# Strassen units in a half of the up-projection, late loads on GpSimd's queue and the gate's sigmoid at the pair's end, in a one-core decoder layer on Trainium2

## The chip, the cores and the metric

The kernel runs on one core of a Trainium2 chip. A core has five engines that run side by side, each with its own queue of instructions: TensorE (PE in the profile; PEld is its loading of weights) multiplies matrices, VectorE (DVE) and ScalarE (ACT) work element by element, GpSimd (POOL) does small odd jobs, and SyncE (SP) only starts transfers. Sixteen DMA engines move data between HBM and the on-chip memory SBUF; both SP and POOL start such transfers here. Matmul results land in the accumulator memory PSUM, in banks of 512 columns. The metric is the device time of one execution, in microseconds, as the median of several runs.

## What is computed

One layer of a decoder trunk in fp32, with 512 tokens and a model width of 2048. The part that matters here is the middle line of this excerpt, the up-projection of two branches with their gates:

```python
h = rmsnorm(x, attn_norm_g[i])
proj = h @ w_in[i]                        # u | v_sgu | q | k | v_att | g_a | g_b
...
y_a = chunked_spatial_gating(u, v_sgu, w_s[i], b_s[i]).reshape(B, S, SGU_WIDTH)
...
y_b = stick_breaking_attention(q, k, v_att).reshape(B, S, SB_WIDTH)

merged = jax.nn.sigmoid(g_a) * (y_a @ w_up_a[i]) + jax.nn.sigmoid(g_b) * (y_b @ w_up_b[i])
x = x + merged @ w_o[i]

h = rmsnorm(x, ffn_norm_g[i])
hid = h @ w_ffn_in[i]
...
x = x + (jax.nn.silu(gate) * up) @ w_ffn_out[i]

ple = p[i] @ w_ple[i]
x = x + jax.nn.sigmoid(rmsnorm(x, ple_norm_g[i]) @ w_ple_gate[i]) * ple
```

`y_a` and `y_b` are 1024 wide, the gates `g_a` and `g_b` 2048 wide. The row factor of the first norm is left out of the in-projection's operands and multiplied into its results afterwards.

## The kernel before

**Data layout.** Everything is transposed: features stand on the 128 partitions, the 512 tokens along the columns. A block of 256 features is held as 1024 columns (two halves of 512). Each fp32 operand is split into a high part `hi` (rounded on ScalarE, L286 for operands, L359 for weights) and a low part `lo` (the rest, on VectorE, L287 and L356), and a product is three matmuls, high by high, high by low and low by high (`mm3`, L289 to L298).

**Units and pairs.** A *unit* is one 256 by 256 block of weights against one operand block. A *pair* (`pair`, L807, and class `Pair`) makes one 256-feature block of output, summed over all units; `doubles` takes units two at a time. A unit is of one of two kinds. Kind "P" (plain) multiplies the four 128 by 128 blocks directly, 12 matmuls of 512 columns, into two PSUM banks, y and z. Kind "S" is one Strassen step (in Winograd's form) over feature halves and token halves: seven products of three matmuls with 256 columns each, 21 in all, into four banks; `mix` (L709) combines the products on ScalarE and VectorE. With `doubled` set, and no P unit in the pair, a different order of the S products is used, with 512 columns in two of the three terms (L687 to L694).

**Weights.** `plan` lists the weights in the order of use, `Weights` brings them. A landing buffer (four of them) receives each entry by SP (L339 for P, L341 and L343 for S). An S entry of two units comes as 256 KB and 384 KB; GpSimd then adds a further 256 KB onto it while loading (L363, an accumulating load); VectorE makes two more sums (L375), and both engines split the blocks. `prepare_early` and `prepare_late` run these steps for entries one to four ahead of the one in use.

**Operands.** A `Form` is an operand block on its way from a raw load to its split parts. `plain_form` (L613) holds the two parts for P units alone. `late_form` (L599) first builds what P units need (`plain_first`, L532) and later, from a second load of the same block, the sums and differences that S units need. Two arenas in SBUF, `parts` (split operands, eight *places* of 3584 columns and 1024 more) and `wholes` (raw blocks), give out space by hand with `take` and `give`. `now` (L830) turns an S unit into a P unit while the output index j is below that unit's entry in a bounds list; so the first pairs of a stage run plain, until the second loads are in.

**The order of the work.** `tick` (L209) is called every one or two units while TensorE's instructions are written out: at each tick at most one operand load is asked for, one form is begun, one second load is asked for, and the callbacks put off by `after(n, ...)` run. What a tick writes is held behind the latest matmuls on its engine, and each engine and each queue executes in the order written.

**The stages.** The in-projection (eight operand forms that fill all places) makes in turn q, k, v and 14 of the 16 gate blocks, with the attention's steps between, then the spatial gating's blocks s and u, then the last gate blocks a7 and b7. Each gate block is stored raw to HBM (`gate_spill`, L1327). `y_b` is stored too (`y_spill`); `y_a` stays in `wholes`. The up-projection (L1350 to L1374) runs j = 0 to 7, and for each j first the b half, then the a half, four P units each. It loads the gate block by SP, scales it by the norm's row (`scaled`, L1222) and takes the sigmoid (L1357) one tick after the pair begins, and multiplies the pair's two banks into it (L1362). The sum of both halves is stored as "mix". Between the j come pairs for the embeddings (`ple_pair`). Then follow the output projection (`w_o`), the FFN's two projections and the last gate. Their operands are spilled to HBM between stages and come back through `spilled_form` (L1338), all with `load` (L516) on SP's queue.

The two places of the code that the change's parts turn on:

```python
        for b in "ba":
            plan((w_up_a if b == "a" else w_up_b)[j], "PPPP")      # L1276
...
            after(1, gate)                                          # L1359
            pr = pair([ys[b, i] for i in range(4)], last=j == KU - 1)
            for h, ps in zip((g[:, :T], g[:, T:]), pr.ends()):
                nc.vector.tensor_tensor(out=h, in0=h, in1=ps, op=ALU.mult)
```

## Time and profile before

| What | Value |
|---|---|
| Median of 3 runs | 2661.22 us (2660.4 to 2664.61) |
| Profiled execution, its time | 2659.74 us |
| Profiled execution, its span | 2658.0 us |
| Granted TensorE clock, mean | 0.999 |
| DMA traffic | 559.77 MB, mean 211 GB/s |

How to read the profile: its page gives the busy time of each engine, the chain of work that ended last followed back from the end, and the costliest groups of instructions. A row such as `L356 DVE TENSOR_TENSOR wlo<-wholes,whi ... x22 | 26.9, 1223 | 29.8 <-ACT whi L359 29.7` is a group: source line, engine, operation, what it writes and reads, count, busy us, mean ns of one, then the time its engine stood idle just before, and for whom. A view of waits says who waited for whom, in us, with the number of times and the longest one. A view by stretches gives busy time and counts between two moments; an instruction that began before the stretch is counted in it too. Matmuls are pipelined: each lasts longer than the step from one start to the next, so TensorE's pace is read from starts.

### The profile page before, as it was taken

The numbers are of one execution on the slowest core, as the hardware profiler recorded it, in microseconds if no ns is written. First come the engines' busy times: TensorE is split into PE (matmuls) and PEld (weight loads), VectorE is DVE, ScalarE is ACT, GpSimd is POOL, SyncE is SP. The second block draws the span as 40 slices with busy tenths as digits, with TensorE's granted clock in tenths as the row PEclk, the third lists the DMA queues.
The fourth block names the chain that finished last, engine by engine and source line by source line (L and its number), as shares of the span: only waits on it lengthen the run. The fifth ranks groups of instructions, "written<-read, shape, count | busy, mean of one in ns | idle before, by whom it ended". The sixth has DMA issues, their size and how long they took to land.

```text
span 2658.0 us, 42554 instructions
## 1 busy us (share of the span) xinstructions
PE 2638.2 (99%) x15336; PEld 2312.3 (87%) x15336; DVE 2234.6 (84%) x3821; ACT 1403.2 (53%) x2233; POOL 448.1 (17%) x556
## 2 busy tenths in 40 slices
PE   8999999999999999999999999999999999999999
PEld 7888888888998888888888888888888888889898
DVE  8687878787886558999888888888889989989876
ACT  7756565655554334566444444444445445455543
POOL 0122222232220001101111111111110211211110
PEclk9999999999999999999999999999999999999999
DMA  7677777777775668978888888788887989978884
GB/s 229 162 194 171 192 173 191 172 191 179 178 191 183 232 212 268 265 236 218 223 210 216 206 200 203 194 209 204 199 207 221 257 227 273 229 229 260 256 240 123
DMA packets 293459, 559.77 MB, mean 211 GB/s; under 512 B 26368, under 2 KB 140544, under 8 KB 293248
## 3 DMA queue, kind: packets, MB, share of 16 engines
q1 hardware_dynamic: 231136, 441.95, 50.7%
q0 software_dynamic: 62112, 115.11, 27.5%
q8 instruction: 120, 1.97, 0.3%
q14 instruction: 91, 0.75, 0.1%
HBM read 505.57 MB, written 51.38 MB: 210 GB/s over the span
## 4 chain that ended last, share of the span: by engine, by line
PE 90%; DVE 4%; DMA 3%; issue 1%; ACT 1%; SPq 0%; POOL 0%; ACTq 0%; POOLq 0%; DVEq 0%
PE ps L692 53%; PE ps L298 10%; PE ps L297 9%; PE ps L296 9%; PE small L692 6%; DVE wlo L356 1%; DVE wholes L527 1%; DMA wholes<-w_ffn_out 1%; PE small L1103 1%; PE small L1155 1%; DVE parts L287 1%; PE small L1029 1%; DMA x<-wholes 1%; ACT whi L359 0%; PE small L1214 0%
## 5 line engine op out<-in xcount | busy, mean ns | idle before, releaser
L692 PE MATMUL ps<-parts,whi 128*128 128x512 f32 x4200 | 1409.4, 398 | 1.6 <-DVE out L796 1.0
L359 ACT ACTIVATE whi<-wholes 128x512 fp32r<-128x512 f32 (+2 forms) x940 | 871.5, 941 | 745.8 <-DVE wholes L375 286.6
L356 DVE TENSOR_TENSOR wlo<-wholes,whi 128x512 fp32r<-128x512 f32 (+2 forms) x940 | 979.4, 1076 | 73.7 <-ACT whi L359 73.0
L692 PEld LDWEIGHTS ps<-parts,wlo 128*128 128x128 f32 x4200 | 790.2, 188 | 178.2 <-issue 1.9
L692 PE MATMUL ps<-parts,wlo 128*128 128x256 f32 x4200 | 831.3, 279 | 0.9 <-DVE wlo L356 0.9
L692 PEld LDWEIGHTS ps<-parts,whi 128*128 128x128 f32 x4200 | 677.1, 189 | 10.5 <-issue 3.6
L297 PE MATMUL ps<-parts,whi 128*128 128x256 f32 (+1 forms) x1832 | 605.0, 331 | 0.7 <-DVE parts L287 0.5
L298 PE MATMUL ps<-parts,wlo 128*128 128x256 f32 (+1 forms) x1832 | 604.9, 331 | 0.5 <-DVE wlo L356 0.5
L296 PE MATMUL ps<-parts,whi 128*128 128x256 f32 (+1 forms) x1816 | 597.3, 330 | 7.4 <-ACT parts L286 5.3
L297 PEld LDWEIGHTS ps<-parts,whi 128*128 128x128 f32 x1832 | 347.0, 189 | 39.0 <-DVE parts L287 2.7
L296 PEld LDWEIGHTS ps<-parts,whi 128*128 128x128 f32 x1816 | 343.6, 190 | 40.4 <-ACT parts L286 5.7
L298 PEld LDWEIGHTS ps<-parts,wlo 128*128 128x128 f32 x1832 | 347.3, 190 | 32.4 <-DVE wlo L356 1.6
L375 DVE TENSOR_TENSOR wholes<-wholes 128x256 f32<-128x256 f32 (+1 forms) x820 | 345.0, 421 | 17.9 <-DVE wlo L356 1.4
L751 DVE TENSOR_TENSOR out<-out,ps 128x256 f32<-128x256 f32 x490 | 202.3, 416 | 147.6 <-ACT out L748 147.4
L363 POOL DMA_DIRECT2D wholes<-w_ffn_in x169 | 147.1, 870 | 702.1 <-DVE wholes L375 251.7
L363 POOL DMA_DIRECT2D wholes<-w_in x132 | 116.6, 885 | 531.3 <-DVE wholes L375 132.8
L692 PE MATMUL small<-parts,whi 128*128 128x512 f32 x480 | 190.3, 397 | 0.0
L287 DVE TENSOR_TENSOR parts<-wholes,parts 128x1024 fp32r<-128x1024 f32 (+3 forms) x137 | 122.8, 907 | 18.5 <-ACT parts L286 18.5
L286 ACT ACTIVATE parts<-wholes 128x1024 fp32r<-128x1024 f32 (+3 forms) x137 | 106.5, 800 | 54.2 <-DVE wholes L527 35.7
L748 ACT ACTIVATE out<-ps 128x256 f32<-128x256 f32 x258 | 96.3, 383 | 50.7 <-PE ps L692 46.7
L363 POOL DMA_DIRECT2D wholes<-w_ffn_out x64 | 55.7, 871 | 360.6 <-DMA wholes<-w_ffn_out 89.2
L1402 ACT ACTIVATE out<-out 128x512 f32<-128x512 f32 x44 | 27.9, 633 | 155.6 <-DVE out L1401 155.6
(124 smaller groups left out, 1770.0 us busy)
## 6 DMA issues: line engine op xcount, KB each, us to landing
wholes<-w_ffn_in SPq DMA_DIRECT2D x169, 384.0 KB, 5.5
wholes<-w_in SPq DMA_DIRECT2D x132, 384.0 KB, 5.1
wholes<-w_ffn_in SPq DMA_DIRECT2D x169, 256.0 KB, 4.7
wholes<-w_ffn_in POOLq DMA_DIRECT2D x169, 256.0 KB, 5.3
wholes<-w_in SPq DMA_DIRECT2D x132, 256.0 KB, 4.3
wholes<-w_in POOLq DMA_DIRECT2D x132, 256.0 KB, 5.0
wholes<-w_ffn_out SPq DMA_DIRECT2D x64, 384.0 KB, 6.3
wholes<-x SPq DMA_DIRECT2D x45, 512.0 KB, 5.8
```

Of the source, the lines that this page charges most:

```text
L286: return (nc.scalar.activation(hi, src, AF.Copy), nc.vector.tensor_tensor(out=lo, in0=src, in1=hi.bitcast(F32), op=ALU.subtract))
L287: nc.vector.tensor_tensor(out=lo, in0=src, in1=hi.bitcast(F32), op=ALU.subtract))
L296: nc.tensor.matmul(ps, sh, mh, start=start, stop=False)
L297: nc.tensor.matmul(ps, sh, ml, start=False, stop=False)
L298: return nc.tensor.matmul(ps, sl, mh, start=False, stop=stop)
L356: in_turn(nc.vector.tensor_tensor(out=self.lo[:, blocks], in0=r, in1=h.bitcast(F32), op=ALU.subtract))
L359: in_turn(nc.scalar.activation(h, r, AF.Copy))
L363: nc.gpsimd.dma_start(out=raw[:, 3:5], in_=self.src[:, 1:3], accum_op=ALU.add)
L375: in_turn(nc.vector.tensor_tensor(out=o, in0=x, in1=y, op=ALU.add))
L692: m = nc.tensor.matmul(out, l, r, start=first and k == 0, stop=last and k == 1)
L748: in_turn(nc.scalar.activation(out, x, AF.Copy, scale=scale))
L751: in_turn(nc.vector.tensor_tensor(out=out, in0=x, in1=y, op=op))
```

## The change

1. `w_up_b`'s units become Strassen units after the first one or two j (`UP_UNTIL`), and y_b's forms `late_form`. For j = 0 the order is a, then b; from j = 1 on b, then a, as before.
2. Gate blocks are scaled by the norm's row two ticks after their pair, before the spill. The sigmoid is written at the end of the up pair. A pair with S units is multiplied in from SBUF in one operation.
3. The loads of gate blocks, of y_b and of all spilled operands (first and second ones) go by GpSimd's queue.
4. Space is given back earlier: the attention's tiles after the last spatial-gating block, the norm's row three ticks into the up-projection. The first part of y_a's first form lies in the 1024 columns at the top of `parts`.

```diff
+UP_UNTIL = 1, 1, 2, 2
...
-    def load(src, n=1024, how="old"):
+    def load(src, n=1024, how="old", queue=nc.sync):
         b = take(n, how)
-        nc.sync.dma_start(out=b.f(0, 1024), in_=src)
+        queue.dma_start(out=b.f(0, 1024), in_=src)
...
     def plain_form(src, ready=always, gain=None, raw=1024, how="low", far=False):
+        hows = [how] * 2 if isinstance(how, str) else how
+
         def steps(form):
-            hi, lo = form.blocks = parts.take(1024, how), parts.take(1024, how)
+            hi, lo = form.blocks = [parts.take(1024, h) for h in hows]
...
                 op0=ALU.mult, op1=ALU.add)
+        if rnd == 3:
+            assert ("b", 3) in y_done
+            give(*att.values())
+            att.clear()
...
         for j in range(KU):
-            for b in "ba":
-                plan((w_up_a if b == "a" else w_up_b)[j], "PPPP")
+            for b in "ba" if j else "ab":
+                plan((w_up_a if b == "a" else w_up_b)[j],
+                     "PPPP" if b == "a" else now("SSSS", UP_UNTIL, j))
...
     def y_form(c, i):
-        return plain_form((lambda: y_a[i]) if c == "a" else lambda: load(y_spill[i]),
-                          lambda: len(y_done) == 8, raw=0 if c == "a" else 1024,
-                          far=c == "b")
-
-    ys = {(c, i): y_form(c, i) for c in "ba" for i in range(4)}
+        def ready():
+            return len(y_done) == 8
+
+        if c == "a":
+            return plain_form(lambda: y_a[i], ready, raw=0, how="low" if i else ("high", "low"))
+        return late_form(lambda size=1024: load(y_spill[i], size, queue=nc.gpsimd), ready, far=True)
+
+    ys = {(c, i): y_form(c, i) for c in "ab" for i in range(4)}
...
-            d = tc.dram_tile([P, 1024], F32, name=nm("gsp"))
-            nc.sync.dma_start(out=d, in_=o)
-            gate_spill[w, i] = d
-    finish_waiting()
-    give(*att.values())
+            d = gate_spill[w, i] = tc.dram_tile([P, 1024], F32, name=nm("gsp"))
+
+            def spill_gate(o=o, d=d):
+                scaled(o, row1)
+                nc.sync.dma_start(out=d, in_=o)
+
+            after(2, spill_gate)
+    after(3, lambda: give(norm1.block))
...
     def spilled_form(kind, n, j, gain=None, **how):
         return (late_form if kind == "S" else plain_form)(
-            lambda size=1024: load(spill[n, j], size), lambda: (n, j) in there, gain, far=True,
+            lambda size=1024: load(spill[n, j], size, queue=nc.gpsimd), lambda: (n, j) in there, gain, far=True,
             **how)
...
     for j in range(KU):
-        for b in "ba":
-            s = load(gate_spill[b, j], 1024, "low")
+        for b in "ba" if j else "ab":
+            s = load(gate_spill[b, j], 1024, "low", nc.gpsimd)
             g = s.f()
-
-            def gate(g=g):
-                scaled(g, row1)
-                nc.scalar.activation(g, g, AF.Sigmoid)
-
-            after(1, gate)
-            pr = pair([ys[b, i] for i in range(4)], last=j == KU - 1)
-            for h, ps in zip((g[:, :T], g[:, T:]), pr.ends()):
-                nc.vector.tensor_tensor(out=h, in0=h, in1=ps, op=ALU.mult)
-            if b == "b":
+            pr = pair([ys[b, i] for i in range(4)], last=j == KU - 1, j=j,
+                      until=UP_UNTIL if b == "b" else None)
+            nc.scalar.activation(g, g, AF.Sigmoid)
+            if pr.n["S"]:
+                tt(g, g, pr.out(), ALU.mult)
+            else:
+                for h, ps in zip((g[:, :T], g[:, T:]), pr.ends()):
+                    tt(h, h, ps, ALU.mult)
+            if j not in part:
                 part[j] = s
...
-    give(norm1.block)
```

More of the change, by code (lines that the diff above doesn't have):

```diff
@@ L630, in steps @@
             yield
-        return Form("P", steps, [(parts, 1024, how)] * 2 + [(wholes, raw, "low")] * bool(raw),
+        return Form("P", steps, [(parts, 1024, h) for h in hows] + [(wholes, raw, "low")] * bool(raw),
                     ready, src, far)
```

## The prediction

> **What bounds the kernel now.** I read the page's busy line and chain of waits first, then busy time by stretches, then who made TensorE wait.
>
> ```profile
> PE 2638.2 (99%) x15336; PEld 2312.3 (87%) x15336; DVE 2234.6 (84%) x3821; ACT 1403.2 (53%) x2233; POOL 448.1 (17%) x556
> ...
> PE 90%; DVE 4%; DMA 3%; issue 1%; ACT 1%; SPq 0%; POOL 0%; ACTq 0%; POOLq 0%; DVEq 0%
> ```
>
> TensorE is busy 99% of the span and carries 90% of the chain. Its matmuls are pipelined, so the busy share alone says little; what counts is how many it starts per microsecond. The next view gives that by stretch (us, then busy time and instructions of PE, PEld, DVE, ACT, POOL, then granted clock, DMA share, GB/s). The up-projection is 815 to 1005 us.
>
> ```profile
> 815.00:840.00 25.00, 24.25 (x106) 19.21 (x105) 20.92 (x26) 15.40 (x16) 0.00 (x0) 1.00 0.58 184
> 840.00:1005.00 165.00, 165.00 (x729) 136.70 (x728) 89.60 (x97) 57.39 (x64) 0.88 (x1) 1.00 0.63 214
> ...
> 100.00:600.00 500.00, 498.94 (x3157) 443.30 (x3156) 406.56 (x759) 319.20 (x681) 130.91 (x195) 1.00 0.73 183
> 815.00:1005.00 190.00, 189.25 (x834) 155.91 (x833) 110.52 (x122) 72.79 (x80) 0.88 (x1) 1.00 0.62 210
> 1005.00:1160.00 155.00, 154.03 (x866) 133.78 (x866) 142.70 (x244) 79.70 (x107) 21.99 (x25) 1.00 0.91 261
> ...
> 1250.00:2000.00 750.00, 750.00 (x4303) 655.06 (x4302) 665.57 (x1195) 359.17 (x498) 133.98 (x154) 1.00 0.83 206
> ```
>
> From 840 to 1005 us TensorE starts 728 matmuls (729 less one begun before), all plain ones of 512 columns: 165/728 = 0.2267 us each, without a gap. VectorE is busy 54% there, ScalarE 35%, GpSimd once. So this stage is bound by TensorE alone, and by nothing but the number of its matmuls. The first 25 us are worse: at that pace 25 us hold 110 starts and the one begun before, and there are 106, so 5 or 6 starts, some 1.3 us, are lost. The clock is 1.00 in all of them.
>
> Who TensorE waited for, in three stretches (us in total, times, longest): 100 to 800, 800 to 1005, and from 1005 on.
>
> ```profile
> PE small L1214 <- ACT wholes L1052: 2.2, 1, 2.2
> PE small L1103 <- ACT wholes L1052: 1.0, 3, 0.4
> ```
> ```profile
> PE ps L297 <- DVE parts L287: 0.5, 1, 0.5
> PE ps L296 <- ACT parts L286: 0.2, 1, 0.2
> ```
> ```profile
> PE ps L692 <- DVE out L796: 1.0, 2, 0.8
> PE ps L692 <- DVE wlo L356: 0.9, 1, 0.9
> PE ps L298 <- DVE wlo L356: 0.5, 1, 0.5
> PE ps L692 <- ACT whi L359: 0.4, 1, 0.4
> PE ps L692 <- DVE out L751: 0.2, 1, 0.2
> ```
>
> Little is left to win from waits: 3.0 us in the last 1650 us, and at the up-projection's start the operands' split (L286, L287), which comes late.
>
> **The change, part by part.** *Strassen units.* The stage has 64 units and five pairs for the embeddings, each of 12 plain matmuls: 69 x 12 = 828. With the new bounds (1, 1, 2, 2) units 0 and 1 of `w_up_b` are plain for j = 0 alone, units 2 and 3 for j = 0 and 1: 2 x 7 + 2 x 6 = 26 become Strassen units of 7 x 3 = 21 matmuls of 256 columns. `pair` is called without `doubled`, so they run through `mm3` (L296 to L298). Such a stretch in the last part of the down-projection, in order of time (start, duration; 23 rows left out):
>
> ```profile
> 2388.09 0.28 PE L297 MATMUL ps<-parts,whi 128*128 128x256 f32 x1
> ...
> 2390.97 0.28 PE L297 MATMUL ps<-parts,whi 128*128 128x256 f32 x1
> ```
>
> 24 steps in 2.88 us are 0.120 us each. A plain unit takes 12 x 0.2267 = 2.720 us, a Strassen unit 21 x 0.120 = 2.520 us; 26 x 0.200 = **5.2 us less**. It is small because half the columns take 53% of the time, not 50%.
>
> The Trainium skill ("TensorE: Matmul & The Clock Gate", section on the back-to-back issue gap) gives N/2.4 + 2.5 ns for a warm matmul: 215.8 ns and 109.2 ns here, an estimate of 2.590 against 2.293 us a unit, and 7.7 us in all. The trace disagrees in both forms (226.7 and 120 ns), so the rows decide; by the page the forecast would be 2.5 us lower.
>
> *What the Strassen units ask of the others.* Groups in the up-projection (860 to 980 us) and in the output projection (1100 to 1160 us), by shape:
>
> ```profile
> L356 DVE TENSOR_TENSOR wlo<-wholes,whi 128x1024 fp32r<-128x1024 f32 x22 | 26.9, 1223 | 29.8 <-ACT whi L359 29.7
> L359 ACT ACTIVATE whi<-wholes 128x1024 fp32r<-128x1024 f32 x22 | 23.1, 1056 | 28.2 <-PE ps L297 21.2 <-issue 6.2 <-DMA wholes<-w_o 0.9
> L1362 DVE TENSOR_TENSOR wholes<-wholes,ps 128x512 f32<-128x512 f32 x20 | 13.2, 684 | 10.9 <-ACT wholes L1357 5.6 <-PE ps L298 5.2
> L1224 DVE TENSOR_TENSOR wholes<-wholes 128x1024 f32<-128x1024 f32 x10 | 12.2, 1223 | 12.6 <-DMA wholes<-gsp 12.6
> ```
> ```profile
> L356 DVE TENSOR_TENSOR wlo<-wholes,whi 128x1280 fp32r<-128x1280 f32 x12 | 17.8, 1483 | 0.0
> L359 ACT ACTIVATE whi<-wholes 128x1280 fp32r<-128x1280 f32 x11 | 14.0, 1269 | 7.7 <-PE ps L692 4.3 <-DMA wholes<-w_o 3.3
> L375 DVE TENSOR_TENSOR wholes<-wholes 128x256 f32<-128x256 f32 x23 | 9.7, 421 | 0.4
> L363 POOL DMA_DIRECT2D wholes<-w_o x10 | 8.8, 879 | 42.2 <-DVE out L751 18.4 <-DVE wholes L375 11.5 <-DMA wholes<-w_o 6.4
> L356 DVE TENSOR_TENSOR wlo<-wholes,whi 128x512 fp32r<-128x512 f32 x12 | 8.2, 684 | 0.0
> L359 ACT ACTIVATE whi<-wholes 128x512 fp32r<-128x512 f32 x12 | 7.5, 627 | 7.8 <-DVE wholes L375 7.8
> ```
>
> A pair of Strassen units costs VectorE 1.48 + 0.68 + 2 x 0.42 = 3.0 us of weights' work instead of 1.22, ScalarE 1.27 + 0.63 = 1.9 instead of 1.06, and GpSimd one accumulating load (0.88). Thirteen such pairs add 23 us on VectorE, 11 on ScalarE. The mixing (`mix`: five operations of 256 columns at 0.42, one of 512 at 0.68) adds 2.8 us in each of seven b rounds, 20 us. The four b operands' further blocks (some seven operations of 256 to 768 columns, about 2.8 us each by the same rows) add 11. The gate rows' scaling, 16 x 1.22 = 19.5 us, leaves the stage. VectorE: 110.5 + 23 + 20 + 11 - 19.5 = 145 us of a stage of about 184, 79%. From 1250 to 2000 us it is busy 89% and TensorE loses nothing, so I cost all this at **nothing**; were that cover gone, it would be a wait like those of L796 and L356 above, under 1 us each. Strassen weights bring 384 KB more a pair, 5 MB, and 2 MB for the operands' second loads: 39 GB/s on 210; the output projection takes 261 GB/s without harm.
>
> *Start of the stage.* For j = 0 the a half goes first. Its operands are in SBUF, need no load, and fit into what the first two freed input operands leave, and each gives its block back, which makes room for the b operands' loads. Counting ticks, all four a operands are built in the last in-projection pair, b's plain blocks within the first up pair (10.9 us), and b's second loads are asked for there too, one pair before j = 1 needs them. I take the lost starts back: **-1.3 us**; bounds -1.3 (all back) and +3 (a second load of 5.8 us and 2.8 us of VectorE against one plain pair's second half, 5.4 us, if they are asked for only once used).
>
> *Scaling before the spill.* The same 16 instructions of 1.22 us run two ticks after their gate pair, 14 of them between 100 and 600 us, where VectorE rises from 406.6 to 423.7 of 500 us (85%). Queued behind each are weights' splits (L356) and attention's steps, for which TensorE waits. Bounds: 0 (by the 89% stretch) and 19.5 us (each passed on whole). TensorE waited for VectorE nowhere from 100 to 800 us, so I stay near the first: **+0.3 us**. The spill's store leaves SP's queue later, with the whole rest of the stage to land. The sigmoid now comes at the pair's end in ScalarE's order, but needs only its load, asked for one pair (10 us) earlier; were it late, the weights' splits (L359) behind it would wait, and they run a pair ahead. The table load moves behind the operands' splits.
>
> *Loads by GpSimd's queue.* SP's loads by `load` (L518) that move are those of hid, gsp, mix and y, and 29 of the 45 of x (16 for the FFN's operands, 13 for the gate's).
>
> ```profile
> L518 SPq DMA_DIRECT2D wholes<-x x45: 319/327/1256, 1038.8 to 2598.1; - x45
> L518 SPq DMA_DIRECT2D wholes<-hid x42: 319/327/432, 1227.9 to 2369.4; - x42
> L518 SPq DMA_DIRECT2D wholes<-gsp x16: 320/423/1055, 763.9 to 993.4; - x16
> L518 SPq DMA_DIRECT2D wholes<-mix x16: 319/355/912, 849.2 to 1037.4; - x16
> L518 SPq DMA_DIRECT2D wholes<-y x4: 326/326/326, 766.2 to 818.2; - x4
> ...
> DMA to landing us min/median/max: 3.2/5.8/9.6
> ```
>
> With y's second loads 29 + 42 + 16 + 16 + 8 = 111 loads move. They go in between the weights' accumulating loads (L363), and where a load waits, the next accumulation waits behind it, then the weights' split. How long loads wait now for the store they read, in SP's queue, and what a 512 KB transfer by GpSimd costs (L1438, an accumulation):
>
> ```profile
> SPq L518 <- DMA x<-wholes: 47.8, 16, 6.7
> ```
> ```profile
> L1438 POOL DMA_DIRECT2D x<-out x16: 872/1165/1193, 2063.7 to 2363.2; - x16
> ...
> DMA to landing us min/median/max: 5.3/8.9/10.2
> ```
>
> A moved load takes 0.87 to 1.2 us of GpSimd, and lands between as fast as now (5.8) and 3.1 us later (8.9); I take 0.6 later, nearer to a plain load. Bounds on the path: -3.0 us (every wait after 1005 us goes, as SP is freed for weights) and the rival's price below. The 16 transfers of L1438 already stand between the accumulations, and from 2000 us on TensorE's waits stayed within the 3.0 us listed: **+0.0**.
>
> **Sum.** -5.2 - 1.3 + 0.3 = -6.2 us. It is made against the profiled execution, 2659.74 us (span 2658.0 and 1.74 around it), which gives 2653.5; that execution lay 1.5 us under the median of 2661.22, so the median should become **2655.0**. Its own range, 2652 to 2657.5, is the S-unit pace to 1% and a microsecond or two of waits.
>
> **Rivals.** *Accumulations behind late loads (slower).* Place: the 16 loads of x1 and x2 that follow their own store. Price: 3.0 us of wait (47.8/16), 1.2 of issue and 3.1 of slower landing delay the next accumulation by 7.3 us; a pair of units is 5 us of matmuls, so if the weights have one pair of cover, 2.3 us each, 37 us, 2692 us; if two (10 us), nothing. Half of the 16, those in the output projection with VectorE at 92%, give 18 us: 2673. It decides from 0.8 us a load. Against it: GpSimd idles 83%, and SP's queue bore the same waits. The Trainium skill ("DMA: Bandwidth & Descriptors", sections Specifications, Issuing engine by pattern, and SWDGE vs HWDGE vs iDMA) speaks for it: plain loads belong on SP, and GpSimd writes its descriptors into SBUF, where VectorE can lock it out; its first byte comes 0.4 us later, an estimated 44 us if all 111 stood on the path. No row so far shows a plain load there.
>
> *Late operands (no change).* The b operands' second loads come late after all: +3 on the start, and 1.3 not won: 2655.0 + 4.3 = 2659. For it: L286 and L287 are what TensorE waits for there now.
>
> *Scaling reaches TensorE (no change).* A quarter of 19.5 us: 2655.0 + 4.6 = 2660. Against it: no wait for VectorE in that stretch.
>
> *Later waits go too (faster).* 2655.0 - 3.0 = 2652. Against it: L796 and L356 wait for VectorE at 92%, not for a load.
>
> **How the numbers follow.** Forecast 0.47, accumulations 0.13, late operands 0.16, scaling 0.14, later waits 0.10. A measurement of this kernel tells about 0.2%, 5.3 us, from no change: faster is under 2655.9, slower over 2666.5. The forecast lies 0.9 us inside faster and gives it 0.38, with the later waits and the pace's lower end 0.50; the two middle rivals and the forecast's upper part make 0.36; the accumulations 0.14. The range 2650 to 2667 leaves out most of the last, and little below.
>
> **What would show it.** Right: in the up-projection 516 matmuls of 512 and 546 of 256 columns, the stage some 182.5 us, no wait for L286 or L287 at its start, as many starts as before in 100 to 600 us, and no growth in TensorE's waits after it. Wrong: ScalarE's splits (L359) waiting longer for accumulations, new waits of TensorE for L356 or L359 at the stage changes, waits for VectorE between 100 and 600 us, or 256-column matmuls over 0.125 us.

## The result, and the profile after

| | before | after |
|---|---|---|
| Median of 5 runs each | 2660.4 us (2656.82 to 2664.61) | 2698.47 us (2691.61 to 2701.73) |
| Span of the profiled execution | 2658.0 us | 2696.8 us |
| Mean granted clock | 0.999 | 0.995 |

The ratio is 1.014, 95% interval 1.0129 to 1.0152: the changed kernel is 38 us slower, outside the predicted range. The changed kernel's page, its busy line and the chain by engine and line:

```profile
PE 2647.7 (98%) x15571; PEld 2324.5 (86%) x15571; DVE 2278.6 (84%) x3915; ACT 1421.5 (53%) x2266; POOL 514.5 (19%) x680
...
PE 77%; DVE 9%; DMA 8%; issue 3%; ACT 3%; POOL 0%; SPq 0%; ACTq 0%; POOLq 0%; DVEq 0%
PE ps L695 50%; PE ps L299 6%; PE ps L298 6%; PE ps L297 6%; PE small L695 6%; DVE wlo L357 3%; DVE wholes L528 2%; DMA wholes<-gsp 2%; DMA wholes<-w_ffn_out 2%; DMA wholes<-x 2%; DVE parts L288 1%; DVE out L754 1%; DMA wholes<-hid 1%; ACT whi L360 1%; DVE wholes L376 1%
```

TensorE carried 90% of the chain and now carries 77%. The chain now runs through loads of operands and of the gate rows (gsp, x, hid: 5%) and the splits behind them. Line numbers are somewhat higher than before: L359 is now L360, L518 is L519, L715 is L718. The changed kernel by stretches, in the columns of the prediction's view:

```profile
100.00:600.00 500.00, 498.41 (x3150) 441.36 (x3149) 419.24 (x769) 317.52 (x677) 125.70 (x194) 1.00 0.73 182
...
815.00:840.00 25.00, 24.98 (x127) 21.20 (x126) 23.10 (x39) 15.49 (x20) 3.03 (x6) 1.00 0.77 268
...
860.00:1000.00 140.00, 127.71 (x759) 112.81 (x758) 82.58 (x119) 54.35 (x69) 17.61 (x26) 0.98 0.69 213
...
1000.00:1060.00 60.00, 53.69 (x281) 46.08 (x280) 41.73 (x63) 26.54 (x30) 10.40 (x16) 0.94 0.80 254
...
1280.00:2040.00 760.00, 760.00 (x4361) 663.09 (x4361) 673.25 (x1208) 364.33 (x507) 136.68 (x159) 1.00 0.82 206
2040.00:2240.00 200.00, 195.60 (x1062) 167.50 (x1061) 179.12 (x294) 99.20 (x129) 44.14 (x59) 0.99 0.87 235
```

From 860 to 1000 us TensorE, which had been busy without a gap, stands still for 12 us. From 1280 to 2040 us it stands still nowhere. The losses lie in the up-projection and at the changes of stage, where operands are loaded. Counts change with the mix of shapes, so I made the account from the starts: for each two neighbouring matmuls the step from start to start, less the usual step of that pair of shapes; every excess over 30 ns is summed by stretch (totals were added up before rounding). Us lost by TensorE in the profiled executions, the experiments' included:

| Stretch | before | after | e1 | e4 | e9 | e13 | e7 | e18 | e19 |
|---|---|---|---|---|---|---|---|---|---|
| 0 to 800 | 25.9 | 24.5 | 24.9 | 24.5 | 24.6 | 23.3 | 25.5 | 23.5 | 24.5 |
| 800 to 860 | 1.6 | 0.3 | 0.5 | 0.0 | 0.0 | 0.0 | 2.8 | 2.1 | 1.9 |
| 860 to 1000 | 0.0 | 18.2 | 4.7 | 10.5 | 1.7 | 0.0 | 0.0 | 0.0 | 0.0 |
| 1000 to 1060 | 1.5 | 9.7 | 7.8 | 6.1 | 0.7 | 0.2 | 4.6 | 4.0 | 2.9 |
| 1060 to 2040 | 1.0 | 4.0 | 4.4 | 2.7 | 5.5 | 3.3 | 3.9 | 5.4 | 1.3 |
| 2040 to the end | 4.8 | 22.2 | 17.1 | 4.6 | 5.4 | 6.5 | 25.9 | 12.0 | 25.7 |
| all | 34.6 | 78.9 | 59.3 | 48.5 | 37.8 | 33.2 | 62.8 | 47.0 | 56.3 |

After less before is 44.3 us, and the span is 38.8 us longer: the missing 5.5 us are what fewer columns saved. Of the 44.3, 18.2 + 8.2 = 26.4 us lie between 860 and 1060 us, and 17.4 after 2040 us. Who TensorE waited for:

```profile
PE ps L299 <- DVE wlo L357: 10.2, 9, 3.0
PE ps L298 <- DVE parts L288: 8.6, 6, 4.8
PE ps L297 <- ACT parts L287: 6.9, 3, 5.1
PE ps L297 <- ACT whi L360: 5.1, 3, 2.0
```

Weights' splits and operands' splits are late. Behind them stand the waits of the other engines in the same execution:

```profile
DVE out L721 <- ACT out L718: 76.0, 14, 11.0
ACT wholes L1370 <- DMA wholes<-gsp: 72.2, 14, 9.7
...
POOL wholes L519 <- DVE wholes L1379: 58.3, 5, 18.3
```

L1370 is the sigmoid: ScalarE stands 72.2 us, 14 times, before it for the gate row's load. The mixing of the Strassen products on VectorE (L721) waits 76.0 us for ScalarE's copies (L718). Before, the same two lines were L718 and L715, and the wait came from the other stages' Strassen units alone:

```profile
DVE out L718 <- ACT out L715: 30.0, 10, 4.4
```

And the load itself waited on GpSimd 58.3 us, five times, for the block it is to fill (L1379 is the sum of both halves, after which a block comes free). One such place, GpSimd's, ScalarE's and TensorE's order of time (start, duration, then in brackets the idle time before and its releaser):

```profile
920.44 0.55 POOL L519 DMA_DIRECT2D wholes<-gsp  x1 [13.10 <-DVE wholes L1379]
923.44 0.54 POOL L519 DMA_DIRECT2D wholes<-gsp  x1 [2.44 <-DMA mix<-wholes]
928.87 0.89 POOL L364 DMA_DIRECT2D wholes<-w_up_b  x1 [4.90 <-DMA wholes<-w_up_b]
```

```profile
927.05 1.06 ACT L1370 ACTIVATE wholes<-wholes 128x1024 f32<-128x1024 f32 x1 [6.88 <-DMA wholes<-gsp]
...
932.33 1.06 ACT L1370 ACTIVATE wholes<-wholes 128x1024 f32<-128x1024 f32 x1 [3.27 <-DMA wholes<-gsp]
933.29 1.07 ACT L718 ACTIVATE out<-ps 128x512 f32<-128x512 f32 x2
934.25 0.63 ACT L360 ACTIVATE whi<-wholes 128x512 fp32r<-128x512 f32 x1
```

```profile
926.27 0.28 PE L299 MATMUL ps<-parts,wlo 128*128 128x256 f32 x1
...
935.52 0.50 PE L299 MATMUL ps<-parts,wlo 128*128 128x512 f32 x1 [3.05 <-DVE wlo L357]
```

The b pair's last 256-column matmul starts at 926.27, so its banks could be copied about then. The copies run at 933.29, because two sigmoids stand ahead of them in ScalarE's order, each waiting for its load; the second belongs to a load issued only at 923.44. The weights' split at 934.25 is behind them too, and TensorE stands 3.05 us at 935.52. The sigmoid was written behind the pair, but it does not read the pair's banks, and nothing else ties it to its place. So what was said of the kernel before, that each engine executes in the order written, does not hold for such an instruction.

### The profile page after: what moved, and what is told of

The parts are those of the page before. It is cut to its first block, busy times and chain, and to the rows that moved or that the text cites. A ratio compares the mean times of both kernels' runs of the same rounds, so it can differ in the third digit from the quotient of the medians.

```text
span 2696.8 us, 43274 instructions
## 1 busy us (share of the span) xinstructions
PE 2647.7 (98%) x15571; PEld 2324.5 (86%) x15571; DVE 2278.6 (84%) x3915; ACT 1421.5 (53%) x2266; POOL 514.5 (19%) x680
## 4 chain that ended last, share of the span: by engine, by line
PE 77%; DVE 9%; DMA 8%; issue 3%; ACT 3%; POOL 0%; SPq 0%; ACTq 0%; POOLq 0%; DVEq 0%
PE ps L695 50%; PE ps L299 6%; PE ps L298 6%; PE ps L297 6%; PE small L695 6%; DVE wlo L357 3%; DVE wholes L528 2%; DMA wholes<-gsp 2%; DMA wholes<-w_ffn_out 2%; DMA wholes<-x 2%; DVE parts L288 1%; DVE out L754 1%; DMA wholes<-hid 1%; ACT whi L360 1%; DVE wholes L376 1%
## 5 line engine op out<-in xcount | busy, mean ns | idle before, releaser
L360 ACT ACTIVATE whi<-wholes 128x512 fp32r<-128x512 f32 (+2 forms) x953 | 881.4, 939 | 727.9 <-DVE wholes L376 329.7
L357 DVE TENSOR_TENSOR wlo<-wholes,whi 128x512 fp32r<-128x512 f32 (+2 forms) x953 | 990.3, 1075 | 46.4 <-ACT whi L360 45.5
L695 PEld LDWEIGHTS ps<-parts,wlo 128*128 128x128 f32 x4200 | 789.1, 188 | 180.8 <-DVE wlo L357 2.5
L695 PEld LDWEIGHTS ps<-parts,whi 128*128 128x128 f32 x4200 | 676.6, 189 | 15.4 <-DVE p L754 4.6
L299 PE MATMUL ps<-parts,wlo 128*128 128x256 f32 (+1 forms) x1910 | 619.6, 325 | 10.3 <-DVE wlo L357 10.2
L298 PE MATMUL ps<-parts,whi 128*128 128x256 f32 (+1 forms) x1910 | 619.8, 325 | 8.9 <-DVE parts L288 8.6
L297 PE MATMUL ps<-parts,whi 128*128 128x256 f32 (+1 forms) x1893 | 612.0, 324 | 12.0 <-ACT parts L287 6.9
L298 PEld LDWEIGHTS ps<-parts,whi 128*128 128x128 f32 x1910 | 365.3, 191 | 44.5 <-DVE parts L288 11.5
L299 PEld LDWEIGHTS ps<-parts,wlo 128*128 128x128 f32 x1910 | 365.5, 191 | 40.9 <-DVE wlo L357 13.8
L297 PEld LDWEIGHTS ps<-parts,whi 128*128 128x128 f32 x1893 | 361.7, 191 | 42.0 <-ACT parts L287 8.0
L376 DVE TENSOR_TENSOR wholes<-wholes 128x256 f32<-128x256 f32 (+1 forms) x846 | 356.6, 422 | 27.9 <-issue 6.4
L287 ACT ACTIVATE parts<-wholes 128x1024 fp32r<-128x1024 f32 (+3 forms) x143 | 111.0, 798 | 55.6 <-DVE wholes L528 40.5
```

Of the source, the lines that this page charges most:

```text
L287: return (nc.scalar.activation(hi, src, AF.Copy), nc.vector.tensor_tensor(out=lo, in0=src, in1=hi.bitcast(F32), op=ALU.subtract))
L297: nc.tensor.matmul(ps, sh, mh, start=start, stop=False)
L298: nc.tensor.matmul(ps, sh, ml, start=False, stop=False)
L299: return nc.tensor.matmul(ps, sl, mh, start=False, stop=stop)
L357: in_turn(nc.vector.tensor_tensor(out=self.lo[:, blocks], in0=r, in1=h.bitcast(F32), op=ALU.subtract))
L360: in_turn(nc.scalar.activation(h, r, AF.Copy))
```

## The experiments

All times are medians; a ratio is to the kernel before on the same chip. The runs were made on several chips, so a difference of a few us between two of them is given by their ratios too; each ratio's interval is about 2.5 us to either side, or wider.

**e1_sigmoid_in_turn.** `in_turn` (L316) makes an instruction follow the last one so marked on its engine, and the next one so marked follow it; the copies L718 and the splits L360 are marked, the sigmoid was not.

```diff
-            nc.scalar.activation(g, g, AF.Sigmoid)
+            in_turn(nc.scalar.activation(g, g, AF.Sigmoid))
```

> The changed kernel with one edit: the sigmoid (L1370) is tied behind the pair's mixing copies on ScalarE. In the changed kernel it stands ahead of them in ScalarE's program although it is written at the pair's end, waits there 72.2 us in all for the gate rows' loads, and the copies (L718) come up to 11 us late. Theory A (that place is what costs in the up-projection): of the 27 us that TensorE loses between 850 and 1050 us most goes, 15 to 25 us, time 2673 to 2683; VectorE's wait for L718 falls from 76 us to under 40. Theory B (the loads on GpSimd's queue hold up the weights' accumulations and the operands everywhere): nothing or under 5 us, 2693 to 2698. Theory C (the Strassen units are too much work for this stage): under 5 us as well. The operands' loads stay on GpSimd, so the 17 us more lost after 2050 us stay by all three.

2678.46 us, ratio 1.0068 (1.0053 to 1.0083): 20 us of the 38 gone by one marker. ScalarE's and VectorE's waits in this run:

```profile
DVE out L721 <- ACT out L718: 30.2, 12, 4.4
ACT wholes L1370 <- DMA wholes<-gsp: 20.6, 7, 7.0
```

The copies' delay is back at the 30 us of before, and ScalarE's order shows why:

```profile
918.24 0.60 ACT L718 ACTIVATE out<-ps 128x512 f32<-128x512 f32 x1 [1.50 <-PE ps L299]
919.68 0.60 ACT L718 ACTIVATE out<-ps 128x512 f32<-128x512 f32 x1 [0.84 <-PE ps L299]
922.75 1.06 ACT L1370 ACTIVATE wholes<-wholes 128x1024 f32<-128x1024 f32 x1 [2.47 <-DMA wholes<-gsp]
```

The copies wait for TensorE alone and the sigmoid comes after them. The stretch from 860 to 1000 us loses 4.7 us instead of 18.2.

**e2_gate_sp, e3_operands_sp, e4_all_sp.** The loads back on SP's queue, the sigmoid as in the change.

```diff
-            s = load(gate_spill[b, j], 1024, "low", nc.gpsimd)                               # e2, e4
+            s = load(gate_spill[b, j], 1024, "low")
-        return late_form(lambda size=1024: load(y_spill[i], size, queue=nc.gpsimd), ...      # e3, e4
+        return late_form(lambda size=1024: load(y_spill[i], size), ...
-            lambda size=1024: load(spill[n, j], size, queue=nc.gpsimd), ...                  # e3, e4
+            lambda size=1024: load(spill[n, j], size), ...
```

> The changed kernel with the 16 gate rows' loads back on SP's queue. Theory A (the sigmoid's place on ScalarE): the load waits for its block in either queue (it was freed by the sum of the j before), so the sigmoid goes on holding up ScalarE: 0 to 8 us less, 2690 to 2698. Theory B (GpSimd's queue makes the loads late, behind accumulations): most of the 27 us lost between 850 and 1050 us goes, 2673 to 2680. Theory C (Strassen units): no change.

2683.78 us, ratio 1.0089 (1.0074 to 1.0104): 15 us less than the change, between the two theories' ranges. The gate rows' queue counts, beside the sigmoid's place.

> The changed kernel with the late operands' loads (y, mix, x1, hid, x2) back on SP's queue; the gate rows' loads stay on GpSimd. Theory B (queue): the 17 us more that TensorE loses after 2050 us and some 3 between 1050 and 1250 go, 15 to 22 us less, 2676 to 2683, and the losses between 850 and 1000 us stay. Theory D (those late losses come from the shift in time that the longer up-projection brings, not from the queue): they stay, 2694 to 2699.

2674.36 us, ratio 1.0053 (1.0036 to 1.0069): 24 us less, somewhat more than theory B's 15 to 22. From 2040 us on TensorE loses 3.3 us, less than the 4.8 before, so the late losses came from these loads.

> The changed kernel with every load back on SP's queue. What is left is the Strassen units, the order a then b at the start, the scaling before the spill and the sigmoid's place. If gate rows' and operands' queues are the whole loss (theory B): 2653 to 2658. If the sigmoid's place costs on its own (theory A): 2668 to 2680, with most of the loss between 850 and 1050 us left. If the Strassen units cost (theory C): the same time as by A, but with TensorE waiting for weights' splits though ScalarE does not wait for gate rows.

2665.32 us, ratio 1.0018 (1.0009 to 1.0027): 33 us less, between the ranges of theories A and B. ScalarE still waits for the gate rows as long as in the change:

```profile
ACT wholes L1370 <- DMA wholes<-gsp: 68.1, 15, 8.5
DVE out L721 <- ACT out L718: 61.4, 17, 7.1
```

So most of that wait is not the queue's doing. Tying the sigmoid behind the copies is worth 6 us from here (e6) and 20 us from the change (e1); why the same wait costs less with the loads on SP was not traced.

**e6_in_turn_all_sp.** e4 and e1 together.

> The changed kernel with every load back on SP's queue and the sigmoid tied behind the pair's mixing copies on ScalarE. With the loads alone on SP it took 2665.3 us and TensorE still lost some 15 us between 860 and 1060 us, with ScalarE waiting 68 us for gate rows and VectorE 61 us for the mixing copies behind them. If the sigmoid's place on ScalarE makes that rest (theory A), 6 to 12 us go: 2653 to 2659, faster than the kernel before. If the Strassen units' own needs make it (theory C), 2662 to 2666.

2659.17 us, ratio 0.9991 (0.9981 to 1.0). The gains of e1 (20) and e4 (33) are not additive: together 39 us. What is left of the change is no longer slower.

**e8_plain_units.** The change without the Strassen units, all else kept.

```diff
-                     "PPPP" if b == "a" else now("SSSS", UP_UNTIL, j))
+                     "PPPP")
...
-        return late_form(lambda size=1024: load(y_spill[i], size, queue=nc.gpsimd), ready, far=True)
+        return plain_form(lambda: load(y_spill[i], queue=nc.gpsimd), ready, far=True)
...
-                      until=UP_UNTIL if b == "b" else None)
+                      until=None)
```

> The changed kernel without its Strassen units: w_up_b's units stay plain for all j and y_b's forms plain; the sigmoid's place, both queues and the scaling before the spill stay as changed. No mixing copies stand behind the sigmoid then, and no accumulations before the gate rows' loads. By theory A (the sigmoid holds up the mixing copies and the weights' splits) most of the loss between 850 and 1000 us goes though the units' 5.2 us come back: 2675 to 2685, the rest being the operands' queue (17 us). By theory B alone (the queue delays gate rows, whatever stands behind the sigmoid) it is 2695 to 2703.

2683.05 us, ratio 1.0082 (1.0067 to 1.0097). The change's other parts cost 23 us without the units, and 15 more with them. Plain pairs need no copies, so a late sigmoid holds up less. TensorE loses nothing from 860 to 1000 us here, though ScalarE still waits 45.3 us for gate rows.

**e9_in_turn_all_sp_old.** e6, and the gate row goes into the space that was given back longest ago ("old") instead of the lowest free one, which is often the one just freed.

```diff
-            s = load(gate_spill[b, j], 1024, "low")
+            s = load(gate_spill[b, j])
```

> The kernel with every load on SP and the sigmoid tied behind the mixing copies, and the gate row's block taken from the space that was freed longest ago, not the lowest, so that its load need not wait for the sum and the store of the j before. If the load's wait for its block is what makes the gate rows late, ScalarE's wait for them falls under 10 us in all and the time is 1 to 4 us under that of the version without this edit: 2651 to 2657. If they are late for SP's queue itself, nothing changes.

2654.49 us (2648.84 to 2658.56), ratio 0.9977 (0.9967 to 0.9986): faster than both kernels, by 6 and by 44 us. In its view of waits no engine waits for a gate row. The same stretches in this run:

```profile
860.00:1000.00 140.00, 139.03 (x848) 125.00 (x847) 95.09 (x133) 66.22 (x81) 9.67 (x11) 1.00 0.75 240
1000.00:1060.00 60.00, 59.70 (x327) 51.70 (x327) 54.95 (x92) 32.16 (x42) 7.95 (x9) 1.00 0.96 294
```

**e14_all_sp_old, e13_best_plain_units, e15_best_gate_pool.** e9 without one of its parts: without the sigmoid's marker; without the Strassen units (as e8); with the gate rows' loads by GpSimd's queue.

> The fastest version so far (2654.5 us) without the tie of the sigmoid on ScalarE: it stands wherever the program's order puts it. If the gate rows now come early enough, its place does not matter: 2653 to 2657. If the place matters even so, 2657 to 2661.

2661.36 us, ratio 1.0007 (0.9998 to 1.0017): 6.9 us over e9 (about 8 by the ratios), ScalarE again waiting 59.3 us for gate rows. The marker counts even with every load on SP and the gate row's space free early.

> The fastest version so far (every load on SP, sigmoid behind the mixing copies, gate rows into the space freed longest ago; 2654.5 us) without its Strassen units: plain units for all j and plain forms. The prediction priced 26 Strassen units at 5.2 us less, from 0.2267 and 0.120 us a matmul: 2658 to 2661. If the units cost nothing but these matmuls, the difference is 4 to 6.5 us; under 2 us and the units are not what makes that version fast.

2658.3 us, ratio 0.9996 (0.9986 to 1.0005): the units by themselves are worth 3.8 us by the medians, about 5 by the ratios.

> The fastest version so far (2654.5 us) with the 16 gate rows' loads on GpSimd's queue, as in the change; their block is free when they are asked for. If the queue alone makes them late (an accumulation that waits for its weights stands ahead of them), ScalarE waits 10 to 30 us for them in all and the time is 2656 to 2662; if only the wait for the block mattered, 2653 to 2657.

2660.78 us, ratio 1.0003 (0.9994 to 1.0012): 6.3 us over e9 (about 7 by the ratios), in the range that was set for late gate rows. But its profiled execution (span 2654.8) was the shortest of ten and lost no more than e9's, and ScalarE waits for no gate row in it. So the cause of this loss is not shown.

**e7_before_operands_pool.** The kernel before with the 91 loads of mix, hid, y and 29 of x by GpSimd's queue, and nothing else changed.

```diff
-    def load(src, n=1024, how="old"):
+    def load(src, n=1024, how="old", queue=nc.sync):
...
-        nc.sync.dma_start(out=b.f(0, 1024), in_=src)
+        queue.dma_start(out=b.f(0, 1024), in_=src)
...
-        return plain_form((lambda: y_a[i]) if c == "a" else lambda: load(y_spill[i]),
+        return plain_form((lambda: y_a[i]) if c == "a" else lambda: load(y_spill[i], queue=nc.gpsimd),
...
-            lambda size=1024: load(spill[n, j], size), lambda: (n, j) in there, gain, far=True,
+            lambda size=1024: load(spill[n, j], size, queue=nc.gpsimd), lambda: (n, j) in there, gain, far=True,
```

> The kernel before with one edit: the late operands' loads (y, mix, x1, hid, x2; first and second ones) by GpSimd's queue, everything else as before: no Strassen units in the up-projection, gate rows by SP, the sigmoid one tick after the pair begins. If that queue alone costs the waits after 1050 us (theory B), it is 10 to 20 us slower than before: 2670 to 2680, with TensorE's losses at the starts of the stages after 2050 us. If they need the changed up-projection (theory D), it stays within 3 us: 2658 to 2664.

2688.48 us, ratio 1.0102 (1.0087 to 1.0118): 28 us by the queue alone, more than the 10 to 20 expected. GpSimd's and ScalarE's order of time in the last part of the down-projection, and TensorE's wait:

```profile
2423.21 0.55 POOL L518 DMA_DIRECT2D wholes<-x  x1 [1.30 <-DMA x<-wholes]
2429.95 0.86 POOL L363 DMA_DIRECT2D wholes<-w_ffn_out  x1 [6.18 <-ACT parts L541]
2430.51 0.86 POOL L518 DMA_DIRECT2D wholes<-x  x1
```

```profile
2438.10 1.34 ACT L522 ACTIVATE wholes<-wholes,gcol 128x512 f32<-128x512 f32 x2 [7.19 <-DMA wholes<-x]
2439.34 1.26 ACT L359 ACTIVATE whi<-wholes 128x1280 fp32r<-128x1280 f32 x1
```

```profile
2444.66 0.58 PE L298 MATMUL ps<-parts,wlo 128*128 128x256 f32 x1 [3.50 <-DVE wlo L356]
```

The same place in the kernel before, SP's queue and ScalarE:

```profile
2401.61 0.39 SPq L341 DMA_DIRECT2D wholes<-w_ffn_out  x1
...
2404.47 0.33 SPq L518 DMA_DIRECT2D wholes<-x  x1
```

```profile
2409.07 1.34 ACT L522 ACTIVATE wholes<-wholes,gcol 128x512 f32<-128x512 f32 x2 [0.28 <-DMA wholes<-x]
```

Before, the load of x left SP 2.9 us after its neighbour's weights and was waited for 0.28 us. In e7 it stands at once behind an accumulating load (L363) that had waited 6.18 us, and ScalarE waits 7.19 us, the weights' split behind it included. Two things make this load late: by its place among TensorE's matmuls it starts 5.1 us later than before, and it lands 7.6 us after its issue, against 4.6. The second is not the rule: a load's issue takes 0.55 us where nothing is in front, and the 91 loads land 0.5 us later than the same ones before, on the mean (6.4 against 5.8 us). Loads of hid and x on the two pages (KB each, median us to landing), e7's and then before's:

```profile
wholes<-hid POOLq DMA_DIRECT2D x42, 512.0 KB, 6.5
wholes<-x POOLq DMA_DIRECT2D x29, 512.0 KB, 5.7
```

```profile
wholes<-x SPq DMA_DIRECT2D x45, 512.0 KB, 5.8
wholes<-hid SPq DMA_DIRECT2D x42, 512.0 KB, 5.6
```

By their place among TensorE's matmuls, the 16 loads that start at once behind an accumulation come 2.3 us later than before on the mean (up to 6.2), the other 75 0.3 us. By the same measure the 278 accumulations from 1000 us on start no later than before on the mean (0.0 us); only four are more than 3 us late. So loads suffer behind accumulations here, and not the other way round.

**e12_operands_pool_wait4.** e7, and an operand's first step is written four ticks after its load was asked for, not two (`WAIT`, L42), so that a slow landing would hold up nothing.

```diff
-AHEAD, WAIT = 3, 2
+AHEAD, WAIT = 3, 4
```

> The kernel before with the late operands' loads on GpSimd's queue (2688.5 us in the run without more) and one constant changed: a form is begun four ticks after its load was asked for, not two, so ScalarE and VectorE reach the operand's instructions some 5 us later and do other work until then. If late loads cost because those instructions wait for them in order, ahead of the weights' splits (theory E), half or more of the 28 us goes: 2662 to 2674. If they cost because the weights' accumulations come late on GpSimd (theory B as first put), the time stays: 2685 to 2691. The four ticks can also push operands too late for their first pair, which would make it slower than 2690.

2693.6 us, ratio 1.0124 (1.0109 to 1.0139), 5 us worse than e7. That is outside both theories' ranges, on the side that the last sentence allows for. The longer wait moves the loss and does not lower it: TensorE's wait at L298 for the weights' splits (L356) falls from 7.3 to 0.2 us, but it waits more for the operands' own splits (L286 12.1 and L287 10.5 us in all, 9.9 and 5.1 in e7).

**e16_before_late_sums, e17_operands_pool_late_sums.** The kernel before and e7, each with the accumulations written one unit later.

```diff
-        for w in list(prepared)[2:]:
+        for w in list(prepared)[2:3]:
             w.to(1)
```

> The kernel before with the accumulating loads placed on GpSimd's queue one unit later (in its line of prepared units the third one alone, not all from the third on). Both theories expect little: the weights' accumulations come later, so that TensorE can meet a late weight here and there, 2660 to 2670 us. It is the base for e17_operands_pool_late_sums.

> e7 (the kernel before with the late operands' loads by GpSimd's queue, 2688.5 us) with the same later place of the accumulations. Theory A, the loads wait in order behind accumulations which themselves wait for their weights' landing: with the accumulations entering later they wait less, and this kernel lies less than 15 us above e16_before_late_sums. Theory B, GpSimd's queue is slower as such for these loads: still 25 to 30 us above it.

2660.23 and 2688.0 us, ratios 1.0 (0.999 to 1.0009) and 1.0104 (1.0089 to 1.0119): 28 us apart, as theory B has it. But the edit missed its aim: in e17 still 15 loads start at once behind an accumulation, 2.2 us late on the mean. It decides nothing.

**e18_front_by_sp, e19_behind_by_pool.** e7 with the loads divided by hand: the 16 that in e7 start at once behind an accumulation and four that follow such a load at once, 20 in all (`BEHIND` lists them), and the other 71.

```diff
...
+        if queue is nc.gpsimd:
+            if (len(operands) in BEHIND) == True:      # e19: == False
+                queue = nc.sync
+            operands.append(src)
         queue.dma_start(out=b.f(0, 1024), in_=src)
```

> e7 (2688.5 us) with the 20 loads that stood behind a waiting accumulation back on SP's queue, and the other 71 on GpSimd's. Theory A, the loads wait in order behind accumulations which wait for their weights' landing: most of the 28 us goes, 2661 to 2670 us; new loads may come to stand behind accumulations, which would leave a part. Theory B, GpSimd's queue is slower as such: 71 of 91 loads are left on it, so about 28 x 71 / 91 = 22 us are left, 2680 to 2685 us.

2677.91 us, ratio 1.0067 (1.005 to 1.0083): 19 us over the kernel before, between the two theories' ranges.

> The other way round: only those 20 loads by GpSimd's queue, the other 71 on SP's. Theory A: most of the loss stays, 2676 to 2688 us. Theory B: 28 x 20 / 91 = 6 us, 2664 to 2670 us.

2679.46 us, ratio 1.0073 (1.0058 to 1.0088): 21 us for 20 loads. This is in theory A's range; B's six are far off. From 2040 us on TensorE loses 25.7 us, as much as with all 91 in e7 (25.9); ten of the 20 start at once behind an accumulation, 3.2 us late. So the wait in order is a cause, and a dear one: 1.05 us for each of these loads, 0.27 for each of the others. But the 71 others cost 19 us too, while only three of them stand at once behind an accumulation and the 71 are 0.55 us late on the mean. Their profiled execution (2672.03 us) lies 6 us under their median, so its column accounts for 12 of the 19 us; why these loads cost so much stays open. The two parts' sum of 40 us is over the 28 of e7, so the two costs do not add; that one delay is partly hidden behind another would explain it, but was not shown.

## Why the prediction was wrong, step by step

*Strassen units, -5.2 us: right in the matmuls.* There are 235 more matmuls (15571 less 15336) against 26 x 9 = 234 expected, and they keep the pace: in the changed kernel

```profile
923.75 0.28 PE L299 MATMUL ps<-parts,wlo 128*128 128x256 f32 x1
...
926.27 0.28 PE L299 MATMUL ps<-parts,wlo 128*128 128x256 f32 x1
```

21 steps in 2.52 us, 0.120 each. The gain shows as 5.5 us between lost time and span. In a frame without the other faults (e9 against e13) it is 3.8 us by the medians and about 5 by the ratios.

*"So I cost all this at nothing": half right.* VectorE and ScalarE had the room (e9: 95.09 and 66.22 of 140 us). From 860 to 1060 us e9 loses 2.2 us more than e13, so the extra work costs TensorE about 2 us in these two executions, where each instruction stands in its right place. What the step left out is that the units bring the copies L718 into ScalarE's order, and so turn a late sigmoid from harmless (e8, 860 to 1000 us: 0.0 lost) into 18.2 us.

*Start of the stage, -1.3: right.* 1.6 us lost there became 0.3, and from 815 to 840 us TensorE is busy 24.98 of 25; it waits for no operand's split there. The rival "Late operands" falls for the b operands' second loads, its place.

*Scaling before the spill, +0.3: right within what the trace can tell.* Up to 800 us TensorE loses 24.5 us against 25.9. From 100 to 600 us it starts 3150 matmuls, where as many as before (3157) were forecast; 7 starts are some 1 us. The rival "Scaling reaches TensorE" (4.6 us) falls.

*"The sigmoid now comes at the pair's end in ScalarE's order, but needs only its load, asked for one pair (10 us) earlier": the first failed step.* Both halves were wrong. On the chip it did not stand at the pair's end but ahead of the pair's copies, since nothing held it there. And to ask for a load is not to have it: GpSimd waited up to 18.3 us for the block that the load was to fill. The prediction named the splits L359 behind a late sigmoid and then costed the step at zero, by the date of the asking. The marker alone is worth 20 us in the change (e1), 6 with all loads on SP (e4 to e6) and 6.9 in e9.

*"Loads by GpSimd's queue, +0.0": the second failed step.* The sizes were fair in e7: 0.55 us of GpSimd where 0.87 to 1.2 was taken, and landing 0.5 us later on the mean where 0.6 was taken. In the change itself the loads land later still: the median of hid is 7.5 us (5.6 before), of mix 7.7 (5.9). But the step failed by its mechanism, which was looked at from the wrong side. I asked what an accumulation suffers behind a late load; the profile shows loads that suffer behind accumulations (e7: 2.3 us against 0.0), and these wait by design, for the sums and splits that set a landing buffer free and for their weights' landing. GpSimd's longest waits in the kernel before:

```profile
POOL wholes L363 <- DVE wholes L375: 466.4, 98, 21.9
...
POOL wholes L363 <- DMA wholes<-w_ffn_in: 133.2, 40, 7.1
```

That GpSimd idled 83% of the span was taken as room; much of it was the queue's head, waiting: its page gives 702.1, 531.3 and 360.6 us of idle time before the accumulations of three weights, of 2210 idle in all. Price: 28 us alone (e7), 24 within the change (e3). The slower rival had the queue, the stages and the order of size (18 to 37 us) and got 0.13; its direction was reversed, so what it had right of the size was luck. How the 28 us divide between the wait in order and the rest stays open (e18, e19). The Trainium skill's rule ("DMA: Bandwidth & Descriptors", SWDGE vs HWDGE vs iDMA), that plain loads belong on SP, came out right here. The 0.4 us of first byte that the same page gives (Specifications) does not explain it: the 20 loads of e19 cost 1.05 us each.

*The sum.* Right terms: -5.2 - 1.3 + 0.3. Missing terms: about 20 us for the sigmoid's place and 24 for the operands' queue, with the gate rows' queue (15 alone) overlapping both; together 44 between the change and e9, of which the gate row's space is 4 to 5 (e6 to e9).

## What to carry to other kernels

Before moving a load to an emptier queue, ask what the instruction at that queue's head waits for: a queue that is idle because it waits is not free, and the load inherits the wait. An instruction that depends on none of its neighbours need not stand in its engine's order where it is written, as the sigmoid here did not; tie it there if what follows must not wait for its input. Two such faults hid a small gain that was there: with both mended (and a gate row's space taken from what was freed longest ago) the same change is 6 us faster than before, and 1 us without the parenthesis's edit (e6).

## What the runs showed of the hardware

TensorE's granted clock falls to half after short waits. The changed kernel by stretches around one such place, and around a later one:

```profile
884.60:888.60 4.00, 1.26 (x7) 0.64 (x6) 1.84 (x2) 3.80 (x4) 0.00 (x0) 1.00 0.03 7
889.40:892.80 3.40, 3.40 (x19) 3.40 (x18) 3.37 (x5) 2.55 (x4) 0.17 (x1) 0.52 0.22 70
893.00:897.00 4.00, 4.00 (x36) 4.00 (x35) 2.36 (x3) 0.00 (x0) 0.72 (x2) 1.00 0.90 269
...
2125.10:2128.40 3.30, 3.30 (x12) 2.87 (x12) 3.30 (x7) 0.45 (x1) 0.00 (x0) 0.51 0.81 247
```

```profile
886.78 0.39 PE L297 MATMUL ps<-parts,whi 128*128 128x256 f32 x1 [1.71 <-ACT whi L360]
...
888.30 0.39 PE L299 MATMUL ps<-parts,wlo 128*128 128x256 f32 x1 [1.02 <-DVE wlo L357]
...
2123.37 0.50 PE L695 MATMUL ps<-parts,whi 128*128 128x512 f32 x1 [1.44 <-DVE p L754]
...
2124.85 0.47 PE L695 MATMUL ps<-parts,whi 128*128 128x512 f32 x1 [0.27 <-DVE out L754]
```

After two waits of 1.71 and 1.02 us the clock is 0.52 for 3.4 us, and the stretch holds 19 matmuls where the next one of 4.0 us holds 36. It did so at 2125 us after waits of 1.44 and 0.27 us, and not after the 3.05 us at 935.52, so the wait's length alone doesn't decide. What does is not shown. The Trainium skill ("TensorE: Matmul & The Clock Gate", Part 1: The HAM clock gate) gives half rate after an idle window of about 3.4 us, on windows that run freely. The 3.4 us of half rate agrees; but in these two places TensorE was idle for no 3.4 us on end. Leaving out the first and the last tens of microseconds, such records sum to 24 us in the changed kernel, TensorE being busy some 22 of them, and to 3.4 us before, all busy. At half speed some 9 of the 38 us, an estimate from these figures, are this surcharge on waits, not waits themselves.
